# S5 preparation with its products on VectorE, and the first norm's weights in x^T

## The chip, the cores and the metric

The kernel runs on one core of a Trainium2 chip. The metric is the device time of one execution in microseconds (us): 1074.84 us is the median of three runs of the kernel before, which lie between 1074.09 and 1077.22 us. Busy times, waits and single durations come from one profiled execution; its times are counted from its first instruction.

## The reference

The model is a trunk of two layers on 256 tokens of 1024 channels, in float32. Each layer adds half a SwiGLU feed-forward of the normed stream, then a mixer, then another half feed-forward. The first layer's mixer is an S5 diagonal state-space model, the second's is sparse attention.

```
h = h + 0.5 * swiglu(rmsnorm(h, ffn1_norm[0]), w_in, w_out)     # w_in 1024 x 5632, w_out 2816 x 1024
u = rmsnorm(h, mix_norm[0])
h = h + s5(u)                                                   # 64 groups of 16 channels, 64 states each
...

s5:  dt = exp(log_dt); lam = exp(a * dt)          # complex, 64 groups x 64 states
     z  = (lam - 1) / a;  bb = z * b              # complex, 64 x 64 x 16
     x_t = lam * x_(t-1) + bb u_t                 # scan over the tokens
     y  = Re(c x) + d_skip * u;  y = gelu(y);  y * sigmoid(y @ w_glu)
```

The change concerns what is computed from the S5 parameters alone (lam, its powers, b, c), and how the first feed-forward applies `ffn1_norm[0]`.

## The kernel before

**Feed-forward.** `ffn` (L177) walks over 11 chunks of 256 hidden units. For a chunk, `w_in` gives 8 slabs of 128 x 512, and `w_out` 4 such slabs. All weights come in granules of 1 MB (128 x 2048, four slabs), loaded by SP into one of two `raw` buffers (L69). TensorE multiplies in the type float32r, and each operand is split into hi + lo: `split_half` (L78) takes half a granule (two slabs, 1024 columns), ScalarE writes `whi` (L86 without a gain, one instruction of 1024 columns; L96 with a gain, one instruction for each 512 columns, since every slab has its own column of gains), and VectorE writes `wlo` (L92 or L99, two instructions of 512 columns). There are five buffers of `whi` and five of `wlo`, each for half a granule. `mm3` (L112) issues three matmuls for each slab and token tile, so a chunk has 8 x 2 x 3 = 48 matmuls of `w_in` and 24 of `w_out`. `second(c - 1)` (L200) multiplies the chunk before by `w_out` after `transposed` (L184) has turned its activations.

**Order on the engines.** The program is written in order, and a scheduler places each instruction in its engine's queue by that order and by its own estimate of when the instruction is ready; a queue then runs in order. A `raw` buffer is loaded again when both its halves are split, that is when VectorE is done with the last `wlo` of it.

**x^T.** `Acts.fill` (L152) transposes half a token tile of h on TensorE and splits it into hi (ScalarE, L140) and lo (VectorE, L141), 128 x 512 each. The norm's weights are not in x^T: they are multiplied into the rows of `w_in` by L96 and L99. The kernel starts with four such fills, then chunk 0.

**The S5 preparation.** `s5_prepare` (L251) is a generator. `background` (L166) is called once after chunk 0 and five times in each later chunk (after slabs 1, 3, 5, 7 and at the chunk's end), 51 times in all, and runs `BG1` = 2 of its steps each time. Its ScalarE, VectorE and SP instructions are queued behind the feed-forward's last ones issued so far. The work, in order: exp, sine and cosine for lam on [128, 32] tiles (VectorE, some 60 short instructions); lam squared and cubed (GpSimd); four scaled copies of c into the stationary operand `Cw`, of which three are complex products (`products`, L343: four GpSimd multiplications of 128 x 512 each, and `c_power`, L355: adds on VectorE); four complex products for b in the same manner; `expand` (L412), which spreads b over blocks of 32 columns by turns on ScalarE and VectorE; for each of 8 blocks j, 8 transposes (L432) and 16 small matmuls (L438) on TensorE with copies out; 16 GpSimd copies into `Wi` (L447, L448); and at the end four rotation tables (`cosT`, `sinT`), each three VectorE instructions of 128 x 512, three on ScalarE and one more on VectorE. Before that, `cosT` and `sinT` serve as scratch space.

**After it.** When the last chunk of the feed-forward is done, `S5In.fill` (L472) norms h into the buffer `hy`, which the preparation used as well, and `s5` (L487) runs. `row_rstd` (L134) computes 1/rms with one GpSimd instruction (L137).

Of the kernel before, what the change touches and what calls it, by code (L numbers as in the profile page):

```python
# [9 lines left out]
F32 = mybir.dt.float32  # L10
# [6 lines left out]
P = 128  # L17
# [15 lines left out]
def kernel(ctx: ExitStack, tc: tile.TileContext, A, out):  # L33
# [19 lines left out]
    # ---- constants and gains  # L53
# [10 lines left out]
    # ---- weights: each granule is split exactly into hi + lo parts as it arrives, scaled by the gain of its rows  # L64
# [13 lines left out]
    def split_half(raw, j, w, gain, k0, eng="av"):  # L78
        """eng: which engines round and subtract"""
# [4 lines left out]
        if gain is None:  # L84
            if eh is S:
                Last.act = S.activation(hi, r, AF.Copy)  # L86
            else:
                Last.dve = V.tensor_copy(hi, r)
        for s_ in range(2):
# [29 lines left out]
    def gemm(acc, xT, gen, kts=KT, lead=False):  # L119
        """acc[t] = x[t] @ W over kts slabs; lead: token tile 0 goes first in groups of four slabs"""  # L120
# [8 lines left out]
    # ---- 1/rms of the rows of one token tile of h, from its two halves  # L129
# [14 lines left out]
    # ---- h^T as hi and lo parts, channels on partitions, with 1/rms of its rows  # L144
    class Acts:
        def __init__(self, hc):
            self.h = hc
# [4 lines left out]
        def fill(self, t, kq):  # L152
# [5 lines left out]
            i = split(hi, lo, ps.rearrange("p (j c) -> p j c", j=4))  # L158
# [6 lines left out]

    def background(bg, n):  # L166
        """n steps of other work, queued behind what has been issued so far"""
        if bg is None:
            return
        with ExitStack() as st:  # L170
            for i in (Last.act, Last.dve, Last.dma):
                st.enter_context(tc.issue_after(i.ins))
            for _ in range(n):
                next(bg, None)

    # ---- res += 1/2 SwiGLU(rmsnorm(h)); done(t, half) once a half of token tile t of res is complete
    def ffn(x, gi, w_in, w_out, res, perm=False, bg=None, steps=1, done=None, first=()):  # L177
        with tc.tile_pool(name="ffn", bufs=2) as fp, tc.tile_pool(name="ps_a", bufs=1, space=PSUM) as pa:
# [5 lines left out]
            def transposed(g):  # L184
                """g^T of one chunk, hi and lo, tokens in natural order"""
# [58 lines left out]
    # ---- S5 in chunks of four tokens: discretisation, rotation tables, and stationary operands  # L244
    BG1 = 2
# [3 lines left out]
    LAG = [12, 6]  # L249

    def s5_prepare(kp, sp, W):  # L251
        scr = kp.tile([P, 2048], F32, name="hy")
        slots = [x[:, i * 512:(i + 1) * 512] for x in
                 (scr, W.cosT.rearrange("p g c -> p (g c)"), W.sinT.rearrange("p g c -> p (g c)")) for i in range(4)]
# [21 lines left out]
        nc.sync.dma_start(out=scr[:, 0:1024], in_=A["s5_c"].rearrange("p r c -> p (r c)"))  # L276
# [4 lines left out]
        cidx = nt("cidx", NC)  # L281
        nc.sync.dma_start(out=cidx, in_=A["cidx"])
# [3 lines left out]
        yield  # L286
# [830 lines left out]
```

## Time and profile before

| what | value |
|---|---|
| median of the runs | 1074.84 us |
| span of the profiled execution, first to last instruction | 1070.4 us |
| median minus span | 4.4 us |
| TensorE, VectorE, ScalarE, GpSimd busy | 94%, 66%, 54%, 17% |
| first feed-forward | about 7.9 to 233 us |
| S5 mixer | about 233 to 317 us |

The profile shows no time of the profiled execution apart from its span; the 4.4 us of the table stand for what lies around it. In the rows, PE is TensorE, PEld its weight loads, DVE VectorE, ACT ScalarE, POOL GpSimd and SP the engine that issues most transfers. A view of windows gives the busy time of each engine in a stretch with the number of instructions in brackets, then the granted TensorE clock as a share of full speed, the share of time that the DMA engines are busy, and GB/s. A row of the timeline gives start, busy time, engine, line, operation, and what it writes and reads; "x4" means four instructions one after the other, and the brackets at the end say how long the engine had been idle and what ended it. Two successive instructions overlap a little, so the start of the next lies closer than the duration of one.

### The profile page before, as it was taken

What the parts mean: (1) busy time and instruction counts of PE and PEld (TensorE: products, weight loads), DVE (VectorE), ACT (ScalarE), POOL (GpSimd) and SP (SyncE); (2) the same over time, 40 slices, a digit from 0 to 9 for tenths busy, and PEclk for the clock granted to TensorE, in tenths of its full rate; (3) what the DMA queues carried; (4) which work ended last, traced back from release to release, by engine and by line L of the source; (5) the groups of instructions that cost most, each with busy time, mean ns of one, the idle gap of its engine ahead of it and who ended that gap; (6) DMA issues with size and microseconds to landing.
All of it is one profiled execution on the core that took longest, in us unless ns stands there. A gap on an engine that the chain in (4) does not pass through costs nothing.

```text
span 1070.4 us, 14818 instructions
## 1 busy us (share of the span) xinstructions
PE 1002.3 (94%) x5553; PEld 807.9 (75%) x5553; DVE 708.6 (66%) x1403; ACT 574.7 (54%) x1051; POOL 180.5 (17%) x185
## 2 busy tenths in 40 slices
PE   7978999988879899999999999999977899999998
PEld 6766877876657688887887888887866678888886
DVE  5999755949875465656757555655688866656553
ACT  6443566643335464655665555554786656545451
POOL 6375100305732000000005100000203220000000
PEclk9988999999989999999999999999988999999999
DMA  6553544420328865555464455554303146555551
GB/s 237 183 187 118 197 158 140 163 91 24 137 103 205 331 201 193 197 176 181 170 221 158 158 187 173 191 197 145 100 1 118 40 138 214 170 186 197 185 176 72
DMA packets 27912, 171.74 MB, mean 160 GB/s; under 512 B 4544, under 2 KB 4992, under 8 KB 9024
## 3 DMA queue, kind: packets, MB, share of 16 engines
q1 hardware_dynamic: 26192, 164.77, 44.5%
q0 software_dynamic: 1648, 6.03, 2.2%
q8 instruction: 43, 0.70, 0.3%
q14 instruction: 29, 0.24, 0.1%
HBM read 165.54 MB, written 5.24 MB: 160 GB/s over the span
## 4 chain that ended last, share of the span: by engine, by line
PE 73%; DVE 14%; DMA 4%; ACT 4%; POOL 3%; issue 2%; SPq 0%; ACTq 0%; POOLq 0%; DVEq 0%
PE mm L115 14%; PE mm L116 13%; PE mm L117 13%; PE o L117 7%; PE o L115 7%; PE o L116 7%; DMA raw<-in_w_in_dram 4%; DVE wlo L99 4%; DVE wlo L92 2%; PE tr L190 1%; DVE w L544 1%; ACT whi L96 1%; DVE Pt L906 1%; ACT Pt L895 1%; PE tr L913 1%
## 5 line engine op out<-in xcount | busy, mean ns | idle before, releaser
L99 DVE SCALAR_TENSOR_TENSOR wlo<-raw,gains,whi 128x512 fp32r<-128x512 f32 (+2 forms) x408 | 295.7, 759 | 130.6 <-ACT whi L96 126.7
L96 ACT ACTIVATE whi<-raw,gains 128x512 fp32r<-128x512 f32 (+2 forms) x408 | 267.3, 699 | 187.2 <-PE mm L117 60.8
L115 PE MATMUL mm<-whi,xT 128*128 128x512 f32 (+2 forms) x800 | 313.5, 392 | 4.5 <-ACT whi L96 3.5
L117 PE MATMUL mm<-whi,xT 128*128 128x512 f32 (+2 forms) x800 | 307.1, 384 | 0.0
L116 PE MATMUL mm<-wlo,xT 128*128 128x512 f32 (+2 forms) x800 | 306.8, 384 | 0.3 <-DVE wlo L99 0.3
L92 DVE TENSOR_TENSOR wlo<-raw,whi 128x512 fp32r<-128x512 f32 x192 | 135.0, 743 | 95.3 <-ACT whi L86 95.1
L86 ACT ACTIVATE whi<-raw 128x1024 fp32r<-128x1024 f32 x104 | 108.8, 1057 | 133.6 <-PE mm L117 62.1
L115 PEld LDWEIGHTS mm<-whi,xT 128*128 128x128 f32 x800 | 151.1, 189 | 36.0 <-ACT whi L96 4.8
L117 PEld LDWEIGHTS mm<-whi,xT 128*128 128x128 f32 x800 | 150.9, 189 | 29.8
L116 PEld LDWEIGHTS mm<-wlo,xT 128*128 128x128 f32 x800 | 151.2, 189 | 28.4 <-DVE wlo L99 1.1
L115 PE MATMUL o<-whi,gT 128*128 128x512 f32 x352 | 143.0, 406 | 9.5 <-ACT gT L140 9.5
L117 PE MATMUL o<-whi,gT 128*128 128x512 f32 x352 | 141.6, 404 | 8.1 <-DVE gT L141 7.9
L116 PE MATMUL o<-wlo,gT 128*128 128x512 f32 x352 | 141.4, 402 | 0.0
L115 PEld LDWEIGHTS o<-whi,gT 128*128 128x128 f32 x352 | 67.7, 192 | 27.5 <-ACT gT L140 11.9
L117 PEld LDWEIGHTS o<-whi,gT 128*128 128x128 f32 x352 | 67.6, 192 | 26.3 <-DVE gT L141 10.1
L116 PEld LDWEIGHTS o<-wlo,gT 128*128 128x128 f32 x352 | 67.7, 192 | 15.7
L235 ACT ACTIVATE g<-mm,rs 128x256 f32<-128x256 f32 x88 | 40.7, 471 | 27.7 <-PE mm L117 27.6
L236 DVE SCALAR_TENSOR_TENSOR g<-mm,rs,g 128x256 f32<-128x256 f32 x88 | 41.9, 483 | 19.9 <-ACT g L235 19.4
L141 DVE TENSOR_TENSOR gT<-tr,gT 128x512 fp32r<-128x512 f32 (+1 forms) x55 | 36.4, 661 | 25.9 <-ACT gT L140 25.6
L140 ACT ACTIVATE gT<-tr 128x512 fp32r<-128x512 f32 (+1 forms) x55 | 33.3, 605 | 33.4 <-PE tr L190 26.7
L137 POOL TENSOR_TENSOR rs<-ms,nhalf 128x1 f32<-128x1 f32 x12 | 7.2, 600 | 231.7 <-DVE ms L136 231.6
L895 ACT ACTIVATE Pt<-Pt,mx 128x128 f32<-128x128 f32 (+1 forms) x64 | 28.4, 445 | 6.4 <-DVE mx L890 6.3
(311 smaller groups left out, 1009.1 us busy)
## 6 DMA issues: line engine op xcount, KB each, us to landing
raw<-in_w_in_dram SPq DMA_DIRECT2D x87, 1024.0 KB, 4.9
raw<-in_w_out_dram SPq DMA_DIRECT2D x44, 1024.0 KB, 4.9
raw<-in_w_kv_dram SPq DMA_DIRECT2D x6, 1024.0 KB, 4.8
raw<-in_w_glu_dram SPq DMA_DIRECT2D x4, 1024.0 KB, 4.8
raw<-in_w_o_dram SPq DMA_DIRECT2D x4, 1024.0 KB, 4.9
revd<-rev POOLq DMA_DIRECT2D x8, 384.0 KB, 15.0
raw<-in_w_qg_dram SPq DMA_DIRECT2D x6, 512.0 KB, 3.6
B<-revd POOLq DMA_DIRECT2D x1, 2048.0 KB, 13.2
```

The lines of the kernel that those rows point to most:

```text
L86: Last.act = S.activation(hi, r, AF.Copy)
L92: i = el.tensor_tensor(out=lo[:, c], in0=r[:, c], in1=hi[:, c].bitcast(F32), op=ALU.subtract)
L96: Last.act = S.activation(hi[:, c], r[:, c], AF.Identity, scale=g_)
L99: i = V.scalar_tensor_tensor(out=lo[:, c], in0=r[:, c], scalar=g_, in1=hi[:, c].bitcast(F32), op0=ALU.mult, op1=ALU.subtract)
L115: T.matmul(ps, lhsT=xh, rhs=wh, start=start, stop=False)
L116: T.matmul(ps, lhsT=xh, rhs=wl, start=False, stop=False)
L117: Last.pe = T.matmul(ps, lhsT=xl, rhs=wh, start=False, stop=stop_)
L140: i = S.activation(dst_hi, src, AF.Copy)
L141: V.tensor_tensor(out=dst_lo, in0=src, in1=dst_hi.bitcast(F32), op=ALU.subtract)
L235: Last.act = S.activation(sl, acc[t][:, 0:256], AF.Silu, scale=rs[:, t:t + 1])
L236: Last.dve = V.scalar_tensor_tensor(out=g[:, t, :], in0=acc[t][:, 256:512], scalar=rs[:, t:t + 1], in1=sl, op0=ALU.mult, op1=ALU.mult)
L895: S.activation(Pt[:, r, br], Pt[:, r, br], AF.Exp, scale=-1.0, bias=mx[:, c:c + 1], accum_out=sm[:, c:c + 1])
```

## The change

- `split_half`: without a gain, `wlo` is one VectorE instruction of 1024 columns where it was two of 512. This holds for `w_out` of all four feed-forwards and for `w_glu`; `w_o`, whose lo part is on GpSimd, stays as it was.
- The first feed-forward has no gain on its weights any more (`gi` is None). `Acts(h, 0)` multiplies the gains into x^T: each of the four fills makes four ScalarE and four VectorE instructions of 128 x 128 where it made one of each of 128 x 512. So the 22 granules of its `w_in` take one ScalarE and one VectorE instruction of 1024 columns for each half, where they took two and two of 512.
- `background` runs steps with costs: each `yield` carries a number, and a call runs steps until their sum reaches 1.65, an overshoot being taken off the next call. The costs add up to 83.55, and 51 calls allow 84.15. For the generators of the other stages, which yield nothing, a step costs 1 as before.
- `times` replaces `products`: a complex product is two multiplications of 128 x 1024 and one subtraction and one addition of 128 x 512, all on VectorE. `c_place` writes them into `Cw` with four ScalarE instructions of 64 x 512. lam squared and cubed move to VectorE, b is multiplied by the gains in one VectorE instruction of 1024 columns.
- The two transfers issued by GpSimd (b, 512 KB, and the gains for it, 256 KB) stand earlier; b has a place of its own in `hy`, so it waits for nothing.
- The tables come between the products of c; their last step moves from VectorE to ScalarE.
- `expand` is gone: the whole of `WBT` is filled by 32 ScalarE instructions of 64 x 256, after two GpSimd memsets of 4096 columns. The products of b lie in `Wi` until then, and `Wi` is cleared afterwards.
- For each block j, the small matmuls come ahead of the transposes. The 16 copies into `Wi` end the generator and fall into its last two calls.

```diff
+        if gain is None and el is V:
+            Last.dve = V.tensor_tensor(out=lo, in0=r, in1=hi.bitcast(F32), op=ALU.subtract)
+            return hi, lo
         for s_ in range(2):
...
-            i = split(hi, lo, ps.rearrange("p (j c) -> p j c", j=4))
+            pv = ps.rearrange("p (j c) -> p j c", j=4)
+            if self.gain is None:
+                i = split(hi, lo, pv)
+            else:
+                for j in range(4):
+                    g_ = gains[:, self.gain, kq * 4 + j:kq * 4 + j + 1]
+                    i = S.activation(hi[:, j], pv[:, j], AF.Identity, scale=g_)
+                    V.scalar_tensor_tensor(out=lo[:, j], in0=pv[:, j], scalar=g_, in1=hi[:, j].bitcast(F32), op0=ALU.mult, op1=ALU.subtract)
...
+        Pace.left = min(Pace.left, 0.0) + n
...
-            for _ in range(n):
-                next(bg, None)
+            while Pace.left > 0:
+                Pace.left -= next(bg, n) or 1
...
-    BG1 = 2
+    BG1 = 1.65
...
+        def times(x, y, o, t):
+            for d, y_ in zip((o, t), y):
+                tt(d, x, y_.unsqueeze(1).unsqueeze(3).to_broadcast([P, 2, NG, 16]), ALU.mult)
+                yield 1.25
+            tt(o[:, 0], o[:, 0], t[:, 1], ALU.subtract)
+            tt(o[:, 1], o[:, 1], t[:, 0], ALU.add)
+            yield 1.4
...
+        c_, b_ = (pair(hy[:, i * 1024:(i + 1) * 1024]) for i in range(2))
+        wv = [pair(flat_w[:, i * 1024:(i + 1) * 1024]) for i in range(8)]
...
+        def c_place(m, x):
+            for rows, cc in halves:
+                S.activation(Cw[rows, :, m, 0, cc], x[rows, 0], AF.Copy)
+                S.activation(Cw[rows, :, m, 1, cc], x[rows, 1], AF.Copy, scale=-1.0)
+
+        nc.gpsimd.dma_start(out=hy[:, 1024:2048], in_=A["s5_b"].rearrange("p r c -> p (r c)"))
+        nc.gpsimd.dma_start(out=flat_w[:, 7680:8192], in_=A["s5_gain"])
...
+        for m in (1, 2, 3):
+            yield from table(m - 1)
+            x = wv[m % 2]
+            yield from times(c_, lam[m], x, wv[2])
+            c_place(m, x)
+        yield from table(3)
...
+        tt(b_, b_, gain.unsqueeze(1).to_broadcast([P, 2, NG, 16]), ALU.mult)
+        yield 1.25
+        for m in range(4):
+            yield from times(bb[0] if m else b_, lam[m] if m else (zre, zim), bb[m], wv[4 + m % 2])
+            if m == 1:
+                G.memset(flat_w[:, 0:4096], 0.0)
+        G.memset(flat_w[:, 4096:8192], 0.0)
...
+        for h_ in range(2):
+            gs = slice(16 * h_, 16 * h_ + 16)
             for m in range(4):
+                for rows, cc in halves:
+                    for r in range(2):
+                        S.activation(WB[rows, gs, r, (3, 1, 2, 0)[m], cc], bb[m][rows, r, gs], AF.Copy)
+                    yield 0.5
+        G.memset(Wi, 0.0)
...
-                x = Acts(h)
+                x = Acts(h, 0)
...
-                ffn(x, 0, A["w_in1_0"], A["w_out1_0"], h, bg=s5_prepare(kp, sp, W), steps=BG1, done=x5.fill, first=[raw0])
+                ffn(x, None, A["w_in1_0"], A["w_out1_0"], h, bg=s5_prepare(kp, sp, W), steps=BG1, done=x5.fill, first=[raw0])
```

With these costs the lam steps fall into the first 9 calls, tables and c products into calls 9 to 22, the b products into calls 23 to 32, the spreading into 33 to 38, the blocks j into 38 to 49 and the copies into `Wi` into 50 and 51. In the kernel before every step counts 1, and 12 and 6 empty steps (`LAG`) stand ahead of the first two adds for `Cw`.

More of the change, by code (lines that the diff above doesn't have):

```diff
@@ new lines, in s5_prepare, with pair @@
+        lre, lim = lam[1]
+        yield 0.8
+        def times(x, y, o, t):
[5 more added lines that the diff above has]
+            yield 1.4
+        halves = [(slice(64 * g2, 64 * g2 + 64), slice(16 * g2, 16 * g2 + 16)) for g2 in range(2)]
+        def pair(x):
+            return x.rearrange("p (r g c) -> p r g c", r=2, c=16)
@@ L431, in s5_prepare @@
                     for ri in range(2):
[L432 removed]
+                        T.transpose(ps[:, (i * 2 + ri) * P:(i * 2 + ri + 1) * P], W.WBT[:, 4 * j + 2 * u + i, ri], ident)
                 S.activation(W.WBT[:, 4 * j + 2 * u:4 * j + 2 * u + 2].rearrange("p a b c -> p (a b c)"), ps, AF.Copy)
[L434 to L442 removed]
+                yield 0.8
         for q in range(4):
```

209 lines of the change are left out of this document (73 added, 136 removed).

## The prediction

> **What bounds the kernel now.** I read the windows of 10 us over the first feed-forward first, the only stage in which the preparation runs.
>
> ```profile
> 30.00:40.00 10.00, 10.00 (x47) 8.20 (x46) 9.07 (x32) 5.78 (x9) 0.00 (x0) 1.00 0.57 197
> 50.00:60.00 10.00, 5.39 (x19) 3.90 (x18) 9.87 (x16) 4.21 (x8) 10.00 (x12) 0.86 0.64 211
> 60.00:70.00 10.00, 10.00 (x44) 8.22 (x43) 9.37 (x10) 2.92 (x5) 6.87 (x6) 0.97 0.51 157
> 70.00:80.00 10.00, 6.95 (x30) 5.32 (x29) 9.28 (x10) 4.63 (x9) 7.77 (x6) 0.88 0.59 210
> 80.00:90.00 10.00, 10.00 (x43) 8.18 (x42) 9.87 (x14) 2.51 (x4) 2.92 (x3) 0.95 0.30 105
> 90.00:100.00 10.00, 7.38 (x34) 5.44 (x32) 9.04 (x7) 5.70 (x9) 9.04 (x7) 1.00 0.31 107
> 100.00:110.00 10.00, 7.80 (x22) 6.13 (x23) 9.05 (x14) 2.58 (x8) 5.85 (x4) 0.66 0.57 190
> 110.00:120.00 10.00, 10.00 (x48) 8.28 (x47) 7.34 (x19) 4.93 (x10) 2.35 (x4) 1.00 0.51 173
> ```
>
> PE is full in the first and the last row; holes stand in the six between, with DVE (third pair) at 90% or more and POOL (fifth) busy beside it. In the first row DVE is as full, POOL idle, and PE loses nothing. The holes add up to 4.61 + 3.05 + 2.62 + 2.20 = 12.5 us; the clock below 1.00 costs 0.14 x 5.39 + 0.03 x 10 + 0.12 x 6.95 + 0.05 x 10 + 0.34 x 7.80 = 5.0 us more. The counts give less: 192 instructions in the six rows against 48 in the last, at a pitch of 0.233 us (below) some 43 in 10 us, so (258 - 192) x 0.233 = 15.4 us. I take 16.5 us, between the two, as what can be had.
>
> Next the timeline, for why DVE is full there:
>
> ```profile
> 94.28 5.94 DVE L92 TENSOR_TENSOR wlo<-raw,whi 128x512 fp32r<-128x512 f32 x4
> 95.23 2.97 POOL L260 TENSOR_TENSOR hy<-cosT,s_l2i 128x512 f32<-128x512 f32 x2
> 114.64 2.50 DVE L92 TENSOR_TENSOR wlo<-raw,whi 128x512 fp32r<-128x512 f32 x4
> 42.00 0.75 DVE L99 SCALAR_TENSOR_TENSOR wlo<-raw,gains,whi 128x512 fp32r<-128x512 f32 x1 [0.19 <-ACT whi L96]
> 49.28 0.79 DVE L99 SCALAR_TENSOR_TENSOR wlo<-raw,gains,whi 128x512 fp32r<-128x512 f32 x1
> 50.10 4.24 SPq L70 DMA_DIRECT2D raw<-in_w_in_dram  x2
> ```
>
> The same four instructions take 5.94 us beside GpSimd products and 2.50 us without: each waits about one GpSimd product (2.97 / 2 = 1.49 us). The last three rows show a second cause: one granule's four wlo lie between 42.00 and 50.07, since short preparation instructions stand between them in DVE's queue, and the next load goes out only then. PE pays for both through the two raw buffers:
>
> ```profile
> ACT whi L96 <- DMA raw<-in_w_in_dram: 32.7, 10, 6.8
> PE o L117 <- DVE gT L141: 7.9, 2, 4.6
> ```
>
> **What PE alone needs.** The last feed-forward has no preparation beside it:
>
> ```profile
> 905.90 6.08 SPq L70 DMA_DIRECT2D raw<-in_w_in_dram  x2
> 922.90 6.08 SPq L70 DMA_DIRECT2D raw<-in_w_in_dram  x2
> 920.00:940.00 20.00, 20.00 (x91) 16.34 (x90) 11.70 (x18) 10.24 (x15) 0.00 (x0) 1.00 0.53 186
> ```
>
> A chunk takes 17.0 us with PE full, so 3.40 us for each of the five calls of background, and 5.67 us for a granule.
>
> **The change, term by term.** First DVE, which takes over the products.
>
> ```profile
> L92 DVE TENSOR_TENSOR wlo<-raw,whi 128x512 fp32r<-128x512 f32 x42 | 27.2, 689 | 31.1 <-ACT whi L86 31.1
> 907.59 1.29 DVE L92 TENSOR_TENSOR wlo<-raw,whi 128x512 fp32r<-128x512 f32 x2 [1.72 <-ACT whi L86]
> L236 DVE SCALAR_TENSOR_TENSOR g<-mm,rs,g 128x256 f32<-128x256 f32 x20 | 9.7, 485 | 6.5 <-ACT g L235 6.5
> L141 DVE TENSOR_TENSOR gT<-tr,gT 128x512 fp32r<-128x512 f32 x9 | 6.2, 691 | 2.1 <-ACT gT L140 2.1
> 206.37 0.68 DVE L260 TENSOR_TENSOR WB<-s_t,s_cidx 128x512 f32<-128x512 f32 x1
> L271 DVE SCALAR_TENSOR_TENSOR s_t<-s_t,s_er 128x32 f32<-128x32 f32 x14 | 2.6, 188 | 0.2
> ```
>
> One instruction of 1024 columns has no row. Two of 512 take 1.29 us, the overlap being 2 x 0.69 - 1.29 = 0.09 us; one instruction saves that start at least, so 1.20 us alone and 1.11 behind another; the upper end is 1.29. Operands read by broadcast cost nothing more (0.68 us, the row of L260). A chunk's own work on DVE is then 6 x 1.20 + 2 x 0.49 + 0.69 = 8.9 us, 1.77 for each call (8.1 and 1.62 with overlaps). A complex product is 2 x 1.20 + 2 x 0.69 = 3.8 us (3.4 with overlaps) for 3.9 units of cost, so a call of 1.65 units holds 1.6 us (1.45). In calls 23 to 32 DVE has 3.37 us of work (3.07) in 3.40: 90 to 99%. Calls 9 to 22 mix in tables and lie some 5% lower; the short instructions (0.19 us each, 60 of them) fill the calls before. All other calls leave DVE half free. So it fits, narrowly, in about 24 of 51 calls. In the six rows above DVE did the old work at 90 to 99% and starved PE; now its instructions are not stretched by POOL and a call interposes one or two of them instead of a run of 8 us.
>
> The loop that must close is that of one raw buffer:
>
> ```profile
> raw<-in_w_in_dram SPq DMA_DIRECT2D x87, 1024.0 KB, 4.9
> L86 ACT ACTIVATE whi<-raw 128x1024 fp32r<-128x1024 f32 x22 | 22.9, 1054 | 33.1 <-PE mm L117 13.3 <-DMA raw<-in_w_out_dram 9.6 <-DVE s_et L267 4.6
> L96 ACT ACTIVATE whi<-raw,gains 128x512 fp32r<-128x512 f32 x88 | 59.7, 715 | 46.4 <-DMA raw<-in_w_in_dram 32.7 <-issue 6.1 <-PE o L117 3.6
> L441 ACT ACTIVATE hy<-tr 128x64 f32<-128x64 f32 x8 | 1.7, 212 | 0.0
> L235 ACT ACTIVATE g<-mm,rs 128x256 f32<-128x256 f32 x22 | 9.8, 465 | 4.4 <-PE mm L117 4.4
> ```
>
> 4.9 us to land, 1.05 for the first whi, two wlo of 1.20 and one call's 1.6 between them: 10.0 us, against 2 x 5.67 = 11.3 us for two granules. A call and a half between them still closes. I take 3.5 us as what the full stretch gives back; bounds 0 (five half granules of whi and wlo lie ahead of PE) and 9 (half of the 16.5).
>
> **Start.** Four 128x128 pieces of x^T replace one instruction of 0.60 us on ACT. A piece lies between 0.212 us (64 columns) and 0.465 (256): about 0.34, so 4 x 0.34 less 0.60 is +0.76 us for a fill. A half of weights is cheaper by 2 x 0.715 - 1.054 = 0.38 us, but its first matmul waits for all 1024 columns.
>
> ```profile
> 6.05 0.60 ACT L140 ACTIVATE xT<-tr 128x512 fp32r<-128x512 f32 x1 [3.81 <-PE tr L156]
> 7.13 0.72 ACT L96 ACTIVATE whi<-raw,gains 128x512 fp32r<-128x512 f32 x1 [0.48 <-DMA raw<-in_w_in_dram]
> 7.90 0.80 PE L115 MATMUL mm<-whi,xT 128*128 128x512 f32 x1 [1.04 <-ACT whi L96]
> ```
>
> The first pieces end about when the weights land at 7.13, so the first matmul moves by 1.05 - 0.72 = 0.33 us and the first wlo by 0.8. Over chunk 0 ACT gets 4 x 0.76 - 4 x 0.38 = 1.5 us more. I take +0.7 us, bounds -0.4 (the halves' saving on the path, the pieces hidden) and +1.6.
>
> The Trainium skill, "ScalarE: Activation LUTs", section "What ACT_TABLE_LOAD costs", gives an ACTIVATE 186 ns + 0.833 ns for each column and 93 ns more for each pointer operand; the trace agrees at 512 columns (715 ns with a gain, 280 + 427 by the rule). It speaks against the pieces: 387 ns for one with its gain, so 1.5 us for four before overlaps, and the estimate for the start would be +0.9 instead of +0.7.
>
> **ACT's other new work** is no bound: 32 spreading instructions of 64x256 at 0.34 to 0.465 us are 11 to 15 us in calls 33 to 38, 2 to 2.5 us for each call beside the chunk's own 6 x 1.05 + 2 x 0.465 + 0.6 = 7.8 us, 1.6 a call. That is 3.6 to 4.1 us in 3.40; the 1 to 4 us by which ACT falls behind over six calls are covered by the halves that lie ahead of PE. Without that cover they would be PE's loss; they are inside the 9 us.
>
> **Tail.** The copies into Wi now come last, and the normed h for S5 goes into the same buffer hy behind them; the GpSimd power of row_rstd queues behind them too.
>
> ```profile
> 111.64 2.48 POOL L448 COPY Wi<-hy 32x256 f32<-32x256 f32 x4 [2.97 <-DVE hy L260]
> 186.06 11.00 POOL L447 COPY Wi<-hy 32x256 f32<-32x256 f32 x12 [71.94 <-DVE hy L440]
> 221.67 0.40 PE L115 MATMUL o<-whi,gT 128*128 128x512 f32 x1
> 225.17 0.60 PE L190 MATMUL tr<-ident,g 128*128 128x128 f32 x4
> 231.85 0.56 POOL L137 TENSOR_TENSOR rs<-ms,nhalf 128x1 f32<-128x1 f32 x1 [34.80 <-DVE ms L136]
> ```
>
> Fifteen matmuls between 221.67 and 225.17 give the pitch of 0.233 us. The last block's sums come in call 48, after slab 3 of the last chunk. From there to the transposes at 225.17 PE has 24 + 24 matmuls, 11.2 us, so that point is 214 on this clock; copies from about 215 take 13.5 us, to 228.5; the power is asked for at 231.85. Slack 3.4 us, so I count nothing; bounds 0 and +5 if the last block is late by 8 us.
>
> **S5 and the other feed-forwards.** w_glu's eight halves save 0.09 us each on a busy DVE, but a longer instruction holds the scans back by up to 0.5 us: -0.3, bounds -1.5 and +1.5. In the later feed-forwards DVE is under 60% busy (11.70 of 20 us above) and PE covers the 0.7 us by which the first slab of a w_out half comes later. The b transfer (512 KB) moves to about 8 us, beside loads that are wanted at 16 us: nothing.
>
> **Sum.** 1070.4 - 16.5 + 3.5 + 0.7 - 0.3 = 1057.8 us of span. With the 4.4 us between span and median: 1062.2, I say 1062.
>
> By the Trainium skill, "VectorE: DVE Perf Modes", section "The TRN2 errata", a float32 tensor_tensor takes (N + 151) / 0.96 ns, 1.224 us for 1024 columns; no run here shows one yet. A chunk's call would then hold 3.42 us at most, and the estimate of what is given back would be 4 us instead of 3.5.
>
> **Rivals.**
>
> Half kept (chance 0.17). DVE cannot sustain 90 to 99% with its waits for whi, so calls 9 to 33 run at DVE's pace. For: the six rows, where DVE stood at 90 to 99% too. Against: the window from 30 us, full without POOL, kept PE full. It gives back 9 instead of 3.5 us: 1067.5.
>
> No change (0.09). GpSimd only filled time that DVE now needs for the products: 7 products of 2 x 1.2 us are 17 us new on DVE, as much as the stretching cost. Against: the stretching is 2.50 to 5.94 us for four instructions. 1074.8.
>
> Slower (0.09). The scheduler bunches: it places the units of several calls between the two halves of one granule, as between 42.00 and 50.07. The loop has room for 11.3 - 8.4 = 2.9 us of preparation there. Calls 9 to 33 hold some 14 granules, seven rounds of the two buffers; above 2.9 us each round is late by the excess, and from 5.7 us on the loss (7 x 2.8 = 19.6 us) outweighs the gain. With four calls' share, 6.3 us, it is 7 x 3.4 = 24 us, and 1074.8 - 16.1 + 24 gives 1083. For: it has happened once. Against: a call's share is 1.6 us, and each call is queued behind the half just issued.
>
> **Numbers.** PE-bound with small losses has 0.65: 1062, its own range 1057 to 1067. About 0.3% is what a measurement tells from no change, 3.2 us. Faster takes 0.65 + 0.17 = 0.82, same 0.09, slower 0.09. The range reaches from full recovery (1074.8 - 16.5 - 1.9, with the lower bounds of start and S5: 1056) to beyond half kept, with the tail late: 1072.
>
> **What will show it.** DVE wlo of 1024 columns at 1.2 us and none at 2 us between 50 and 110 us; PE at 10.00 with 43 or more matmuls in those windows and the clock at 1.00; waits of ACT whi for loads in the first feed-forward at a third or less of 32.7 us; the power of row_rstd at about 220 us, not behind a copy into Wi. I am wrong if PE still has holes around calls 9 to 33 with DVE above 95%, or if the feed-forward ends early but S5 begins with a wait for POOL.

## The result, and the profile after

| | before | after |
|---|---|---|
| median of the runs made side by side | 1076.03 us (4 runs, 1074.09 to 1077.44) | 1060.57 us (4 runs, 1057.09 to 1061.47) |
| ratio, 95% interval | | 0.9855 [0.9836, 0.9874] |
| span of the profiled execution | 1070.4 us | 1055.3 us |
| VectorE and GpSimd busy | 66%, 17% | 63%, 13% |

The changed kernel is 1.45% faster, 15.5 us by the medians and 15.1 us by the spans. The run that was profiled was the fastest of its four. For every run listed, time and span lie 1.7 to 2.2 us apart, 1.8 for the four of the kernel after. So the 4.4 us between median and span, before, can't all lie around the execution. The larger part is most likely that the profiled execution was a short one: its 1070.4 us lie below the shortest span listed for that kernel, 1071.7. After, that part is 1060.57 - 1057.09 = 3.5 us. The numbers below are of the two profiled executions unless a median is named.

First the stretch of 50 to 110 us in one row, in the view of windows. The kernel before:

```profile
50.00:110.00 60.00, 47.52 (x184) 37.20 (x183) 56.49 (x66) 22.55 (x39) 42.45 (x35) 0.89 0.49 163
```

The kernel after, the same row and the six rows of 10 us in it that answer to those of the prediction:

```profile
50.00:110.00 60.00, 60.00 (x272) 49.52 (x271) 56.26 (x70) 43.77 (x62) 3.53 (x1) 1.00 0.59 200
...
50.00:60.00 10.00, 10.00 (x46) 8.25 (x45) 9.94 (x17) 7.80 (x12) 0.00 (x0) 1.00 0.55 202
60.00:70.00 10.00, 10.00 (x47) 8.28 (x47) 8.37 (x11) 7.80 (x13) 0.00 (x0) 1.00 0.62 210
70.00:80.00 10.00, 10.00 (x45) 8.23 (x45) 10.00 (x14) 8.35 (x13) 0.00 (x0) 1.00 0.63 210
80.00:90.00 10.00, 10.00 (x48) 8.27 (x47) 9.38 (x12) 7.99 (x12) 3.53 (x1) 1.00 0.61 211
90.00:100.00 10.00, 10.00 (x46) 8.25 (x45) 10.00 (x12) 6.37 (x8) 0.00 (x0) 1.00 0.52 165
100.00:110.00 10.00, 10.00 (x48) 8.24 (x47) 8.58 (x11) 5.46 (x7) 0.00 (x0) 1.00 0.60 206
```

PE has no hole left and its clock is 1.00. VectorE is as busy as before (56.26 against 56.49 us), in two rows all the time, and PE loses nothing by it. Between 91 and 124 us, where the products of b stand, VectorE is busy 31.09 of 33 us, 94% as well, and PE all the time. Between 50 and 110 us PE runs 272 - 184 = 88 matmuls more. At 60 / 272 = 0.2206 us each that is 19.4 us.

How the holes of before came about is seen in its timeline, here at the second of the four:

```profile
76.19 1.33 ACT L96 ACTIVATE whi<-raw,gains 128x512 fp32r<-128x512 f32 x2 [5.37 <-DMA raw<-in_w_in_dram]
77.43 0.57 ACT L140 ACTIVATE gT<-tr 128x512 fp32r<-128x512 f32 x1
78.06 0.79 PE L115 MATMUL o<-whi,gT 128*128 128x512 f32 x1 [3.05 <-ACT gT L140]
```

All four holes (4.61, 3.05, 1.53 and 3.29 us) end with `gT`, the turned activations, and not with the weights themselves. Two of them end with ScalarE's copy of `gT`, which stands in its queue behind a `whi` that waits for a late load, as here. The other two end with VectorE's, which stands behind late `wlo` and the products' adds.

Next the marks by which the span is cut into stages: the first activation of chunk 1, the power of `row_rstd` for S5, and the first of the transfers by which h is reordered at the end of S5 (`hd<-h`). Timeline of before (its power, at 231.85, is in the prediction):

```profile
34.97 0.82 ACT L235 ACTIVATE g<-mm,rs 128x256 f32<-128x256 f32 x2
...
316.27 1.14 SPq L1012 DMA_DIRECT2D hd<-h  x2
```

and of after:

```profile
38.21 0.82 ACT L249 ACTIVATE g<-mm,rs 128x256 f32<-128x256 f32 x2
...
195.85 8.75 POOL L459 COPY Wi<-hy 32x256 f32<-32x256 f32 x12 [49.41 <-DVE hy L445]
213.83 0.55 POOL L140 TENSOR_TENSOR rs<-ms,nhalf 128x1 f32<-128x1 f32 x1 [9.23 <-DVE ms L139]
...
299.18 1.14 SPq L1010 DMA_DIRECT2D hd<-h  x2
```

The start is 3.2 us later. From there to the power it takes 175.6 us instead of 196.9, so 21.3 less. S5 takes 85.4 instead of 84.4. The rest takes 756.1 instead of 754.1. Together, from the times before rounding, 3.2 - 21.3 + 0.9 + 2.0 = -15.1 us. GpSimd had been idle for 9.23 us when the power was asked for, so the copies into `Wi`, which end at 204.6, hold nothing up.

The groups and the waits of after, between 0 and 222 us:

```profile
L90 DVE TENSOR_TENSOR wlo<-raw,whi 128x1024 fp32r<-128x1024 f32 x66 | 80.3, 1223 | 33.9 <-ACT whi L86 33.8
```

```profile
ACT whi L86 <- DMA raw<-in_w_in_dram: 17.5, 8, 4.6
```

One `wlo` of 1024 columns takes 1.223 us. The Trainium skill, "VectorE: DVE Perf Modes", section "The TRN2 errata", gives 1.224 us for it, and the trace agrees. ScalarE's waits for loads of `w_in` fell from 32.7 to 17.5 us.

Last the start, in the timeline of after, and its row in the view of waits between 0 and 24 us:

```profile
6.08 0.37 ACT L167 ACTIVATE xT<-tr,gains 128x128 fp32r<-128x128 f32 x1 [3.84 <-PE tr L159]
6.48 0.35 DVE L168 SCALAR_TENSOR_TENSOR xT<-tr,gains,xT 128x128 fp32r<-128x128 f32 x1 [5.61 <-ACT xT L167]
6.87 0.63 ACT L167 ACTIVATE xT<-tr,gains 128x128 fp32r<-128x128 f32 x2 [0.42 <-DVE xT L168]
7.27 0.61 DVE L168 SCALAR_TENSOR_TENSOR xT<-tr,gains,xT 128x128 fp32r<-128x128 f32 x2 [0.43 <-ACT xT L167]
...
8.31 1.06 ACT L86 ACTIVATE whi<-raw 128x1024 fp32r<-128x1024 f32 x1 [0.82 <-DMA raw<-in_w_in_dram]
```

```profile
ACT xT L167 <- DVE xT L168: 3.3, 5, 1.3
```

ScalarE and VectorE hand the pieces to each other: the second piece on ScalarE (6.87) starts only when VectorE is done with the first (6.48 + 0.35). The first `whi` starts at 8.31 instead of 7.13. The bracket says that the last thing it waited for was the load, for 0.82 us. When the first weights land differs from run to run: in kernels 2 and 12 below, which begin like the kernel after, this `whi` starts at 7.51 and 7.47, without such a wait. So not all of the 3.2 us is the pieces' doing.

### The profile page after: what moved, and what is told of

Read it like the earlier page. It is cut to its first block, busy times and chain, and to the rows that moved or that the text cites. A ratio compares the mean times of both kernels' runs of the same rounds, so it can differ in the third digit from the quotient of the medians.

```text
span 1055.3 us, 14565 instructions
## 1 busy us (share of the span) xinstructions
PE 996.1 (94%) x5553; PEld 806.6 (76%) x5553; DVE 669.9 (63%) x1258; ACT 583.2 (55%) x1039; POOL 135.8 (13%) x142
## 4 chain that ended last, share of the span: by engine, by line
PE 80%; DVE 9%; ACT 4%; DMA 3%; POOL 3%; issue 1%; SPq 0%; ACTq 0%; POOLq 0%; DVEq 0%
PE mm L118 15%; PE mm L119 15%; PE mm L120 15%; PE o L118 8%; PE o L119 8%; PE o L120 8%; DMA raw<-in_w_in_dram 3%; PE tr L204 2%; DVE wlo L102 1%; DVE w L542 1%; DVE Pt L904 1%; DVE wlo L90 1%; ACT Pt L893 1%; POOL z L502 1%; PE tr L911 1%
## 5 line engine op out<-in xcount | busy, mean ns | idle before, releaser
L102 DVE SCALAR_TENSOR_TENSOR wlo<-raw,gains,whi 128x512 fp32r<-128x512 f32 (+2 forms) x320 | 221.4, 730 | 111.7 <-ACT whi L99 108.0
L99 ACT ACTIVATE whi<-raw,gains 128x512 fp32r<-128x512 f32 (+2 forms) x320 | 207.4, 694 | 136.1 <-PE mm L120 58.6
L90 DVE TENSOR_TENSOR wlo<-raw,whi 128x1024 fp32r<-128x1024 f32 x140 | 171.0, 1226 | 122.7 <-ACT whi L86 122.6
L86 ACT ACTIVATE whi<-raw 128x1024 fp32r<-128x1024 f32 x148 | 154.5, 1057 | 153.5 <-PE mm L120 58.2
L118 PE MATMUL o<-whi,gT 128*128 128x512 f32 x352 | 140.5, 399 | 10.9 <-ACT gT L143 10.9
L120 PE MATMUL o<-whi,gT 128*128 128x512 f32 x352 | 138.9, 396 | 0.0
L118 PEld LDWEIGHTS o<-whi,gT 128*128 128x128 f32 x352 | 66.6, 189 | 27.6 <-ACT gT L143 12.6
L120 PEld LDWEIGHTS o<-whi,gT 128*128 128x128 f32 x352 | 66.5, 189 | 16.0 <-DVE gT L144 0.4
```

The lines of the kernel that those rows point to most:

```text
L90: Last.dve = V.tensor_tensor(out=lo, in0=r, in1=hi.bitcast(F32), op=ALU.subtract)
L99: Last.act = S.activation(hi[:, c], r[:, c], AF.Identity, scale=g_)
L102: i = V.scalar_tensor_tensor(out=lo[:, c], in0=r[:, c], scalar=g_, in1=hi[:, c].bitcast(F32), op0=ALU.mult, op1=ALU.subtract)
L118: T.matmul(ps, lhsT=xh, rhs=wh, start=start, stop=False)
L120: Last.pe = T.matmul(ps, lhsT=xl, rhs=wh, start=False, stop=stop_)
```

## The experiments

All were run with the kernel before beside them on the same chip, and each ratio is against that. Its median was 1075.78 to 1076.62 us in these runs. The theory is that the time came from taking the arithmetic that reads SBUF away from GpSimd, because it stretches VectorE's instructions. The rivals are the even pacing, the gains in x^T, and the merged instructions of 1024 columns. The other parts (the tables' and the small matmuls' place, `expand`, the earlier transfers) were not undone alone; run 1 has none of them and run 2 has all. The table puts all runs side by side. The four stages are of the profiled execution, cut at the marks above.

| kernel | start | feed-forward | S5 | rest | span | median us | ratio, 95% interval |
|---|---|---|---|---|---|---|---|
| before | 35.0 | 196.9 | 84.4 | 754.1 | 1070.4 | 1076.03 | 1 |
| after | 38.2 | 175.6 | 85.4 | 756.1 | 1055.3 | 1060.57 | 0.9855 [0.9836, 0.9874] |
| 1: before, memset for products | 34.4 | 180.4 | 84.6 | 756.1 | 1055.5 | 1060.33 | 0.9862 [0.9845, 0.9878] |
| 2: after, products on GpSimd | 36.7 | 188.4 | 85.4 | 762.7 | 1073.1 | 1071.03 | 0.9958 [0.9944, 0.9972] |
| 3: after, two steps a call | 38.3 | 177.1 | 87.0 | 757.2 | 1059.6 | 1059.75 | 0.9856 [0.9841, 0.9870] |
| 4: after, gains in weights | 33.4 | 179.6 | 83.9 | 758.8 | 1055.7 | 1059.94 | 0.9857 [0.9832, 0.9882] |
| 5: after, two of 512 | 37.0 | 179.4 | 84.6 | 759.4 | 1060.5 | 1062.77 | 0.9871 [0.9843, 0.9898] |
| 6: after, ScalarE's pieces first | 35.8 | 176.0 | 87.3 | 759.3 | 1058.3 | 1059.10 | 0.9834 [0.9812, 0.9856] |
| 7: after, fill of three | 34.9 | 175.5 | 83.5 | 759.0 | 1052.9 | 1057.20 | 0.9822 [0.9799, 0.9845] |
| 8: before, copies for products | 36.7 | 183.1 | 86.0 | 757.6 | 1063.4 | 1063.87 | 0.9872 [0.9840, 0.9904] |
| 9: after, S5 mixer on VectorE | 38.4 | 177.9 | 75.6 | 758.1 | 1049.9 | 1051.01 | 0.9758 [0.9737, 0.9780] |
| 10: 7 and 9 together | 35.2 | 177.2 | 74.0 | 757.8 | 1044.1 | 1050.23 | 0.9757 [0.9731, 0.9783] |
| 11: 10, w_o on VectorE too | 35.0 | 175.8 | 75.1 | 754.5 | 1040.4 | 1042.53 | 0.9691 [0.9676, 0.9705] |
| 12: 11 without 7 | 37.4 | 176.3 | 75.2 | 754.5 | 1043.4 | 1047.83 | 0.9733 [0.9710, 0.9756] |

The kernel after and kernels 6, 7 and 9 to 12 have the same feed-forward between the first two marks. They lie between 175.5 and 177.9 us there. That spread of 2.4 us is what a difference in this column has to exceed. In the column of the start, the kernel after and kernels 2, 3, 9 and 12 begin alike and lie between 36.7 and 38.4 us, a spread of 1.7 us.

### 1. Before, without the products' reads

```diff
-                tt(t_, x[i], b16(y[j]), ALU.mult, G)
+                G.memset(t_, 0.0)
```

> The kernel before, with the GpSimd multiplications of the complex products replaced by memsets of the same tiles; the products are left out, all else and the old pacing stay. Theory A (GpSimd's reads and writes stretch VectorE): the holes of TensorE between 50 and 110 us go, wlo of 512 columns takes 0.7 us there, and the time falls by 13 to 20 us, to a ratio of 0.981 to 0.988. Theory B (the unevenness of the old steps made the holes): the holes stay for the most part, the time falls by 6 us at most, ratio 0.994 or above.

The window and the timeline of kernel 1:

```profile
50.00:110.00 60.00, 59.87 (x267) 48.27 (x266) 51.59 (x90) 33.71 (x59) 15.55 (x29) 1.00 0.59 205
```

```profile
88.32 1.41 DVE L99 SCALAR_TENSOR_TENSOR wlo<-raw,gains,whi 128x512 fp32r<-128x512 f32 x2
88.46 1.00 POOL L346 MEMSET hy<- 128x512 f32 x2 [0.20 <-DVE sinT L260]
```

1060.33 us: the whole gain, with the old pacing, the old gains and the old instructions of 512 columns. Two `wlo` beside two memsets take 1.41 us, no more than undisturbed ones (0.75 each in the prediction's rows). So it is what GpSimd reads, not that GpSimd works, that costs VectorE time. The run also shortens the waits of VectorE's adds for the products, so alone it does not part the stretching from those waits. The view of waits does: between 50 and 110 us VectorE waits for GpSimd twice in the kernel before, 2.0 us together, and no such wait stands there in the next run, where the products are on GpSimd again.

### 2. After, with the multiplications back on GpSimd

```diff
-                tt(d, x, y_.unsqueeze(1).unsqueeze(3).to_broadcast([P, 2, NG, 16]), ALU.mult)
+                tt(d, x, y_.unsqueeze(1).unsqueeze(3).to_broadcast([P, 2, NG, 16]), ALU.mult, G)
```

> The changed kernel, with the fourteen multiplications of 1024 columns in the complex products put back on GpSimd; even pacing, 1024-column wlo and gains in x^T stay. VectorE is relieved of 14 x 1.2 us. Theory A: each GpSimd product of some 3 us holds up VectorE's two-input instructions, holes come back, 8 to 20 us slower than the changed kernel, ratio to the kernel before 0.993 to 1.005. Theory B: pacing keeps the holes away, at most 3 us slower, ratio 0.985 to 0.988.

```profile
50.00:110.00 60.00, 55.81 (x235) 44.56 (x234) 51.45 (x66) 39.84 (x58) 23.82 (x9) 0.94 0.52 177
```

```profile
104.61 4.09 DVE L90 TENSOR_TENSOR wlo<-raw,whi 128x1024 fp32r<-128x1024 f32 x2
104.84 2.79 POOL L276 TENSOR_TENSOR Wi<-Wi,s_l1r 128x1024 f32<-128x1024 f32 x1 [2.43 <-DVE Wi L276]
```

1071.03 us over ten runs: 10.5 of the 15.5 us are lost again. In the timeline of kernel 2, two `wlo` take 4.09 us where two in a row undisturbed take at most 2 x 1.223 = 2.45. The difference, 1.6 us, stands beside one multiplication of 2.79 us and the first 1.1 us of the next. VectorE has less to do than in the kernel after (51.45 against 56.26 us busy), and still PE has holes. The stretching is shown from both sides. The other 5.0 us stay; which parts of the change give them was not separated.

How an instruction is held is clearest at a short one of the same kernel:

```profile
48.67 1.95 POOL L276 TENSOR_TENSOR WBT<-hy,s_l2r 128x1024 f32<-128x1024 f32 x1 [0.44 <-DVE s_l2r L276]
48.75 1.92 DVE L276 TENSOR_TENSOR s_t<-s_l2i,s_l1i 128x32 f32<-128x32 f32 x1
```

An instruction of 32 columns, which takes VectorE 0.18 us just before and just after, starts 0.08 us behind a multiplication and lasts until that is done (50.67 against 50.62). GpSimd is held in its turn: such a multiplication takes 1.95 us here and 2.79 us beside the two `wlo`.

### 3. After, with the old pacing

```diff
-            while Pace.left > 0:
-                Pace.left -= next(bg, n) or 1
+            for _ in range(n):
+                next(bg, None)
...
-    BG1 = 1.65
+    BG1 = 2
```

> The changed kernel, with two steps in each call of background whatever they cost (as the kernel before ran them), so that the work is done in 49 of 51 calls but unevenly. Theory A: VectorE has room on average, some 2 to 4 us slower than the changed kernel, ratio 0.988 or 0.989. Theory B: at least half of the gain is lost, ratio 0.993 or above.

1059.75 us, the same as after, and 177.1 us between the marks, inside the spread. The even pacing is worth nothing that can be measured, and the expectation of a loss fell.

### 4 and 5. After, without the gains in x^T, and without the merged instruction

```diff
-                x = Acts(h, 0)
+                x = Acts(h)
...
-                ffn(x, None, A["w_in1_0"], A["w_out1_0"], h, bg=s5_prepare(kp, sp, W), steps=BG1, done=x5.fill, first=[raw0])
+                ffn(x, 0, A["w_in1_0"], A["w_out1_0"], h, bg=s5_prepare(kp, sp, W), steps=BG1, done=x5.fill, first=[raw0])
```

> The changed kernel, with the first norm's weights back in the weights (x^T plain). VectorE gets two instructions of 0.66 us start to start for each half where it has one of 1.14, so 0.18 us more for 44 halves, and ScalarE 0.28 us more. If the pieces of x^T are what costs the start 3 us (activation of chunk 0 at 24.1 and 26.0 us in the changed kernel, 21.2 and 22.6 before), chunk 0 is back at 21 to 23 us; if the start was late for another reason, it stays at 24 to 26. Behind it VectorE is above 100% in calls 23 to 32 by this sum, and 1 to 4 us are lost there. Together -2 to +1 us against the changed kernel.

```diff
-        if gain is None and el is V:
-            Last.dve = V.tensor_tensor(out=lo, in0=r, in1=hi.bitcast(F32), op=ALU.subtract)
-            return hi, lo
```

> The changed kernel, with the wlo of gainless weights as two instructions of 512 columns again, in all stages. VectorE has 0.07 us more for each of 66 halves in the first feed-forward, which would put it at 96% in calls 23 to 32. If VectorE's instruction count matters to the gain, 2 to 4 us slower than the changed kernel; if only the GpSimd products did, within 1 us of it (ratio to the kernel before 0.985 to 0.987).

Neither median (1059.94 and 1062.77 us) can be told from the kernel after: the intervals of the ratios overlap widely. The stages say more. With the gains in the weights the start is 4.8 us shorter, and the feed-forward between the marks is 4.0 us longer. With two instructions of 512 it is 3.8 us longer. So the gains in x^T buy their time in the full stretch and pay it at the start. Both runs split the halves of `w_in` by two `wlo` again, so the 4.0 and the 3.8 us are most likely one effect seen twice. Each of these differences rests on one profile and lies not far outside the spread of 2.4 us.

### 6 and 7. After, with another fill of x^T

Kernel 6 issues the four pieces of ScalarE, then the four of VectorE:

```diff
                 for j in range(4):
-                    g_ = gains[:, self.gain, kq * 4 + j:kq * 4 + j + 1]
-                    i = S.activation(hi[:, j], pv[:, j], AF.Identity, scale=g_)
-                    V.scalar_tensor_tensor(out=lo[:, j], in0=pv[:, j], scalar=g_, in1=hi[:, j].bitcast(F32), op0=ALU.mult, op1=ALU.subtract)
+                    i = S.activation(hi[:, j], pv[:, j], AF.Identity, scale=gs[j])
+                for j in range(4):
+                    V.scalar_tensor_tensor(out=lo[:, j], in0=pv[:, j], scalar=gs[j], in1=hi[:, j].bitcast(F32), op0=ALU.mult, op1=ALU.subtract)
```

> The changed kernel, with the four ScalarE pieces of each x^T fill issued ahead of its four VectorE pieces instead of by turns. ScalarE waited 3.3 us for VectorE between its pieces in the changed kernel's first 30 us. If that exchange is what makes the start late, the activation of chunk 0 comes at 22 to 23 us instead of 24.1, and the time falls by 1 to 2 us; if the weights' landing (8.3 us) makes it late, it stays at 24.

Kernel 7 multiplies the gains in with one VectorE instruction of 512 columns, then splits as without a gain:

```diff
-                for j in range(4):
...
+                n = 2 * (2 * t + kq)
+                xg = W.WBT[:, n:n + 2].rearrange("p a b c -> p (a b) c")
+                V.tensor_tensor(out=xg, in0=pv, in1=gains[:, self.gain, kq * 4:kq * 4 + 4].unsqueeze(2).to_broadcast([P, 4, P]), op=ALU.mult)
+                i = split(hi, lo, xg)
```

> The changed kernel, with each x^T fill as three instructions of 512 columns: VectorE multiplies by the gains (read by broadcast) into scratch, ScalarE rounds, VectorE subtracts. If the start is late through the pieces, chunk 0's activation comes at 21 to 23 us and the time falls by 1 to 3 us; if not, no change.

The start of kernel 6 in the timeline:

```profile
6.13 2.18 ACT L167 ACTIVATE xT<-tr,gains 128x128 fp32r<-128x128 f32 x8 [3.90 <-PE tr L159]
7.31 2.16 DVE L169 SCALAR_TENSOR_TENSOR xT<-tr,gains,xT 128x128 fp32r<-128x128 f32 x8 [6.43 <-ACT xT L167]
8.15 1.10 ACT L86 ACTIVATE whi<-raw 128x1024 fp32r<-128x1024 f32 x1
```

and of kernel 7:

```profile
6.24 0.69 DVE L167 TENSOR_TENSOR WBT<-tr,gains 128x512 f32<-128x512 f32 x1 [5.36 <-PE tr L159]
6.96 0.63 ACT L143 ACTIVATE xT<-WBT 128x512 fp32r<-128x512 f32 x1 [4.72 <-DVE WBT L167]
...
7.50 1.04 ACT L86 ACTIVATE whi<-raw 128x1024 fp32r<-128x1024 f32 x1
```

Eight pieces in a row take ScalarE 2.18 us, 0.27 each, without a wait for VectorE between them, and the first mark comes 2.4 us earlier than in the kernel after, 0.9 us earlier than in the earliest of the five kernels that begin alike. So the handing back and forth was part of the start's delay; how large a part, one profile does not say. With three instructions of 512 the mark is at 34.9, as in the kernel before (35.0), and at 35.2 and 35.0 in kernels 10 and 11, which begin in the same way: three kernels against five, well apart. Kernel 7's median is 3.4 us below the kernel after's, and the intervals just overlap. Kernel 6's, 1.5 us below, can't be told from it.

### 8. Before, with copies that read one operand

```diff
-                tt(t_, x[i], b16(y[j]), ALU.mult, G)
+                G.tensor_copy(t_, x[i])
```

> The kernel before, with each GpSimd multiplication of the complex products replaced by a GpSimd copy of its first operand into the same place, so that the products are left out and GpSimd reads one operand of 512 columns instead of two. The run with memsets in this place gave 1060. If one operand read from SBUF is enough to stretch VectorE's two-input instructions, the wlo of 512 columns beside the copies still takes over 0.9 us and the time stays at 1065 to 1074. If it takes the traffic of a second operand, or the longer duration of the multiplication, wlo stays at 0.69 to 0.75 us and the time is that with memsets, 1058 to 1062. The copies will be shorter than the multiplications (2.97 us for two), so a time between is read by wlo's duration beside a copy and not by the total alone.

```profile
86.23 4.06 POOL L346 COPY hy<-cosT 128x512 f32<-128x512 f32 x4 [0.60 <-DVE cosT L260]
86.69 4.14 DVE L92 TENSOR_TENSOR wlo<-raw,whi 128x512 fp32r<-128x512 f32 x4
```

The same four `wlo` that take 2.50 us alone and 5.94 us beside multiplications take 4.14 us beside copies, over 1 us each. One operand that GpSimd reads is enough. The time, 1063.87 us, is a little under what was named for this outcome and lies between memsets and products, though its interval overlaps with that of the memsets: the copies are shorter than the products, and so is the stretching. The Trainium skill, "SBUF — State Buffer", section "SBUF: two separate sides", says that a VectorE instruction with two inputs from SBUF shares a pair of ports with GpSimd, only against a GpSimd instruction that reads SBUF, and that whichever starts first holds it for the whole of its instruction. Runs 1, 2 and 8 agree with the first part. For the second: from 86.23 to 90.83 the eight instructions take 4.60 us. Less 2.50 for the four `wlo`, that leaves 0.53 us for a copy, near the 1.00 / 2 = 0.50 us of a memset of that size. An estimate only, but it fits engines that take turns, as the short instruction of run 2 does.

### 9. After, with the S5 mixer's arithmetic on VectorE

```diff
-                tt(w[:, 0], w[:, 0], Y[:, 1], ALU.add, V if cb == 0 else G)
-                tt(w[:, 1], w[:, 1], Y[:, 0], ALU.subtract, G)
+                tt(w[:, 0], w[:, 0], Y[:, 1], ALU.add, V)
+                tt(w[:, 1], w[:, 1], Y[:, 0], ALU.subtract, V)
...
-                tt(Y, w, si, ALU.mult, V if cb == 0 else G)
-                tt(z[:, 0], z[:, 0], Y[:, 1], ALU.subtract, G)
-                tt(z[:, 1], z[:, 1], Y[:, 0], ALU.add, G)
+                tt(Y, w, si, ALU.mult, V)
+                tt(z[:, 0], z[:, 0], Y[:, 1], ALU.subtract, V)
+                tt(z[:, 1], z[:, 1], Y[:, 0], ALU.add, V)
```

> The changed kernel, with the additions and multiplications that the S5 mixer itself gives to GpSimd put on VectorE. By the reason found for the first feed-forward (a GpSimd instruction that reads SBUF holds up VectorE's two-input instructions), VectorE gets some 18 us of new work for 43 us of GpSimd time, and its own instructions lose their stretching of about 8 us; it was busy 80 to 90% there. If the stretching and the hand-over between the engines set the pace, 2 to 6 us faster; if VectorE's own work does, 5 to 10 us slower.

Groups of 214 to 290 us, and one window over each kernel's own S5 stage, first the kernel after, with its wait of the scans for GpSimd:

```profile
L542 DVE TENSOR_TENSOR_SCAN w<-r,w 128x64 f32<-128x64 f32 x64 | 16.5, 319 | 8.8 <-POOL w L502 8.7
L502 DVE TENSOR_TENSOR z<-w,cosT 128x512 f32<-128x512 f32 x8 | 6.5, 814 | 0.0
```

```profile
213.83:299.18 85.35, 68.70 (x1050) 55.71 (x1049) 63.21 (x138) 30.72 (x58) 47.31 (x45) 0.90 0.19 65
```

then kernel 9:

```profile
L542 DVE TENSOR_TENSOR_SCAN w<-r,w 128x64 f32<-128x64 f32 x64 | 13.2, 269 | 0.1
...
L502 DVE TENSOR_TENSOR z<-w,cosT 128x512 f32<-128x512 f32 x8 | 5.5, 684 | 0.0
```

```profile
216.24:291.80 75.56, 67.58 (x1050) 55.44 (x1048) 65.12 (x171) 27.32 (x54) 3.21 (x8) 0.93 0.21 72
```

1051.01 us: 9.6 us below the kernel after, and S5 takes 75.6 us where the ten kernels with the mixer's arithmetic on GpSimd take 83.5 us or more. That is more than the 2 to 6 us that were expected. VectorE took over all of that arithmetic and is busy only 1.9 us more over the whole stage. The scans lose their stretching (319 to 269 ns) and their 8.7 us of waiting.

### 10 to 12. The best version

Kernel 10 joins 7 and 9. Kernel 11 adds this, and kernel 12 is 11 with the pieces of the kernel after:

```diff
-            gen = granules([A["w_o"][j] for j in range(KT // 2)], eng='ag')
+            gen = granules([A["w_o"][j] for j in range(KT // 2)], eng='av')
```

> The kernel after with x^T filled by three instructions of 512 columns (alone 1057.2, ratio 0.9822) and with the additions and multiplications of the S5 mixer on VectorE (alone 1051.0, ratio 0.9758). If the two gains lie in stages that do not meet, they add up: the kernel after has the ratio 0.9855, so 0.9822 - (0.9855 - 0.9758) = 0.9725, about 1046 to 1048, with the power of row_rstd near 210.5 and the S5 mixer taking about 76 us. If what is gained at the start is given back in the DMA-bound second feed-forward, as with the gains in the weights, it is no better than the mixer's change alone: 1050 to 1052.

> The kernel with both changes and, besides, the lo part of w_o (16 GpSimd subtractions of 512 columns, 20 us) on VectorE as instructions of 1024 columns. If every GpSimd instruction that reads two operands from SBUF costs the kernel time, this takes off another 1 to 4 us. If it costs only where VectorE is near full, the attention stage with w_o shows no change within 1.5 us, since VectorE has idle time there, or a loss of up to 2 us if VectorE's queue then delays what the attention waits for.

> The kernel of 1042.5 (S5 mixer's and w_o's two-operand GpSimd arithmetic on VectorE, x^T filled by three instructions of 512 columns), with x^T filled by the pieces of 128 columns of the kernel after. The fill of three was worth 3.3 us alone (1057.2 against 1060.57) and nothing beside the mixer's change (1050.2 against 1051.0). If its 3 us at the start reach the end, this gives 1045 to 1046.5, with the power of row_rstd at 213 to 216. If the transfers of the second feed-forward take the start's gain back, it gives 1041.5 to 1044, with the power 2 to 4 us later than 210.85 all the same.

The windows of the stage with w_o, kernel 10 and kernel 11:

```profile
780.00:850.00 70.00, 61.21 (x354) 44.10 (x353) 55.18 (x191) 42.41 (x113) 22.08 (x18) 0.95 0.28 96
```

```profile
780.00:850.00 70.00, 65.64 (x369) 45.99 (x369) 55.66 (x201) 45.13 (x119) 1.76 (x2) 0.98 0.26 91
```

Kernel 11 is the fastest: 1042.53 us, ratio 0.9691 [0.9676, 0.9705], 3.1% below the kernel before. It lies 7.7 us below kernel 10 by the medians and 3.7 us by the spans, where 1 to 4 us were expected at best. In its stage with w_o PE is busy 4.4 us more while VectorE is hardly busier. The last stage falls from 757.8 and 758.1 us (10, 9) to 754.5 in both 11 and 12. Whether this is the stretching once more, or that GpSimd's `wlo` itself comes late for PE, was not separated.

The fill of three against the pieces gave 3.4 us (7 against after), 0.8 (10 against 9) and 5.3 (11 against 12). In the profiles 11 and 12 differ by 2.4 us at the first mark and by 3.0 at the end, so what is won at the start is kept. Kernel 12's median, 1047.83, lies above the 1045 to 1046.5 named for that. The figure expected for kernel 10, 1046 to 1048, was missed by its median, though its four runs reach from 1045.91 to 1052.96.

## Why the prediction was right

Forecast 1062 us, measured 1060.57, and the mechanism was the one named: GpSimd stretched VectorE, and PE starved behind the raw buffers, at its last step through `gT`, whose copies were queued behind the late halves. The terms were less good than their sum.

**Holes, 16.5 us, less 3.5 given back.** Between the marks 21.3 us came, where the two terms together allowed 13.0. Two things failed. The hole term compared the counts with 43 matmuls in 10 us. The kernel after has 272 in six such rows, 14 more than the 258 of the prediction, which is 3.1 us. And the 192 of before, added from rows of 10 us, counted matmuls that cross an edge twice: the one row of 60 us has 184. The holes were 19.4 us. Then the give-back: its lower bound, 0, is what happened. VectorE stood at 56.26 of 60 us, 94%, inside the 90 to 99% that was worked out, and PE did not notice. So VectorE could be near full without a loss here; in run 3, at 58.20 of 60 us, PE lost 0.7 us. That part was right in its working and wrong in the price put on it. In this stage, on one profile each, the runs put 196.9 - 180.4 = 16.5 us (run 1) or 188.4 - 175.6 = 12.8 us (run 2) on the products on GpSimd, about 4 on the shorter split (4 and 5), and nothing on the pacing (3). The prediction had no term for the merged split in the full stretch beyond VectorE's load.

One reading under this term was wrong, though no sum uses it: "each waits about one GpSimd product (1.49 us)". Four `wlo` take 5.94 - 2.50 = 3.4 us longer, so each waits 0.86 us. The 1.49 us are what one `wlo` takes with its wait, and what one product takes with its own.

**Start, +0.7 us (to +1.6).** It was +3.2, outside the bounds. The step that failed added ScalarE's durations, four pieces less one instruction, as if they ran on without a break. The piece was sized well (0.34 us forecast, 0.37 and 0.63 for two in the rows). The load, taken as landing at 7.13 as before, landed at 8.31. What was left out besides is that both engines work on the same tile and wait for each other piece by piece. The Trainium skill's price for a piece ("ScalarE: Activation LUTs", section "What ACT_TABLE_LOAD costs"), 387 ns, agrees with the 0.37 us. The +0.9 worked out from it missed the same wait. Runs 6 and 7 show the wait.

**Tail, 0.** Right: the copies end 9.23 us before the power is asked for, and the power at 213.83 comes earlier than the 220 named.

**S5, -0.3 us, and the rest, 0.** The profiles show +0.9 and +2.0. Kernels with the same S5 as after lie between 83.5 and 87.3 us there. The rest is 754.1 to 757.6 us in before and kernels 1 and 8, which share it, and 756.1 to 762.7 in after and kernels 2, 3, 4, 6, 7, 9 and 10. So S5 can't be judged from one profile, and a loss of some 2 us in the rest is likely but not settled.

**The rivals.** "Half kept" fell: VectorE at 94% and PE full. "No change" fell by the measured time: PE is full while VectorE runs the products, and run 1, which leaves them out with the old splits, is no faster. "Slower" fell too. ScalarE's waits for loads did not fall to a third as the prediction's test asked, but to 54% (17.5 of 32.7 us), the longest 4.6 us. PE is idle for only 0.8 us between the marks (174.82 of 175.62 us busy), so the halves that lay ahead covered these waits, and that test asked for more than the mechanism needs.

**From span to median, 4.4 us.** It was 5.3, of which 1.8 lie around the execution and 3.5 are the choice of the profiled run. No term for that choice is in the prediction. Errors of +2.5 at the start, +1.2 in S5, +2.0 in the rest and +0.9 here, against -8.3 between the marks, sum to -1.7 us: 1062.2 before rounding less 1.7 is the 1060.5 that was measured. That the total came within 2 us is mostly luck: errors that cancelled.

## What to carry to other kernels

GpSimd arithmetic that reads SBUF is not free, even where GpSimd is off the critical path: look at the duration of one two-input VectorE instruction with and without it, and count what the stretching costs before counting what the move adds to VectorE. Where two engines work on one tile, issue all pieces of the first and then all of the second (run 6, one profile), or use wide instructions (run 7, the clearer of the two). When a change has several parts, undo each alone: here one part carried the gain, another (the gains in x^T) won in one stage what it lost in the next, and the pacing was worth nothing that could be measured.

## What was not expected

- VectorE can take over work and hardly be busier: 56.26 us after against 56.49 before between 50 and 110 us, with the products moved onto it, and 65.12 against 63.21 us over the S5 stage for the mixer's whole GpSimd arithmetic (47.31 us of GpSimd time became 3.21).
- GpSimd's memset shows no stretching of VectorE (1.41 us for two `wlo` beside it), its copy does (4.14 us for four), its multiplication more (5.94). A VectorE instruction of 0.18 us took 1.92 us when it came just behind a multiplication.
- Runs of one and the same kernel differ by several us: 1057.09 to 1061.47 in four of the kernel after, 1045.91 to 1052.96 in four of kernel 10, 1073.91 to 1079.78 in the eleven of the kernel before that were run beside kernels 5, 6, 7 and 9. Why is open.
